# GLA and pooling decoder on one core: S as moving operand with its loads a step apart from its stores, first squares without GpSimd, one table set and r in PSUM at the end

## Chip, cores, metric

The kernel runs on one core of a Trainium2 chip. Measured is the device time of one launch in microseconds. TensorE is PE (PEld are its weight loads), VectorE DVE, ScalarE ACT, GpSimd POOL, and SyncE SP; SP issues all DMAs here.

## The reference, cut to what matters

Two layers of a decoder, for a prompt of 256 tokens and 8 samples of 8 tokens each, with the same weights. Everything is float32.

```python
def step(S, inp):                       # GLA, one chunk of the recurrence
    ...
    o_inter = einsum('bhid,bhdv->bhiv', qi * exp(b), S)
    k_dec = ki * exp(b_last - b)
    S_new = exp(b_last)[..., None] * S + einsum('bhjd,bhjv->bhdv', k_dec, vi)
    return S_new, o_intra + o_inter

def trunk(x, ...):
    for l in range(DEPTH):              # DEPTH = 2
        h = rmsnorm(x, norm_mix[l])
        m, s, b = mixer(h, ...)         # w_in, GLA (4 heads) and pooling, w_out
        x = x + m
        h = rmsnorm(x, norm_ffn[l])
        x = x + (silu(h @ w_gate[l]) * (h @ w_up[l])) @ w_down[l]
    return rmsnorm(x, norm_final), ...
```

For the samples each of 8 sequences has a state S of 128 x 256 per head, which is read (o_inter), decayed and added to, and written out; D_MODEL is 2048, D_FF 5632.

## The kernel before

**Layout.** Activations are transposed: channels on 128 partitions, the 320 tokens (256 of the prompt, 64 of the samples) along the free dimension; xT holds 16 such tiles of 320. Each weight value is split into a high and a low part of PE's fast float32 form (hl, two halves of the same tile), and so is the activation (xh, xl); `mm3` makes a product of three matmuls of 128 x 128 weights and 320 columns: high by high (L151), high by low (L152), low by high (L153).

**Units.** The program is a list of some 730 units. A unit is one weight tile of 128 x 1024 (512 KB): a load by SP into one of four raw buffers, a cast on ACT (L115) and a subtraction on DVE (L116) into one of three hl buffers, and eight `mm3`, that is 24 matmuls, on PE. `run` goes over the list: it loads up to five units ahead, splits two ahead, issues a unit's matmuls, then the evacuations due, then lets every generator in `gens` go one step. All engines get their instructions in that order, and each works through its own in order; SP's loads of weights, its loads of S and its stores stand in one queue.

**Small matmuls.** What the mixer needs beside the weight matmuls is queued by `add_small` with an estimated time, and `beside`, called after each `mm3`, puts small ones into the slots between; `placed` lets a generator wait until the queue is empty.

**Heads.** `head_gen` treats one head: loads of the two halves of S (four samples each; two buffers), transposes of v, then per half c of the 256 value channels a PSUM tile ps_o with the products of scores and v (L736, L738, for the samples L740) and, for each of the eight samples, one matmul with S as weights and that sample's eight columns of q8 moving (L743). Then come the new state (L719 into ps_sn, L728 on DVE, store L731), the sum of squares (L763), the prompt's state (L766) and the norm. Heads follow each other; `gate_gen` takes their o to the output projection. The PSUM pool sm has four buffers in turn for all these small tiles.

**Level stage.** Ahead of the heads, `gk_gen` and `level_gen` make the decays and the scores within the prompt; at s == 4 they make e8 = exp of the cumulated gate of the samples' tokens and q8 = e8 times q. `pool_gen` makes the pooling mixer, on POOL for the most part.

**Start.** `first_squares` forms the sum of squares of x over the 16 tiles, for the first norm: products and sums on POOL (L962, L963), two of the four chunks squared by ACT (L969). Meanwhile DVE makes the low parts of weights (L116) and of x (L119). A matmul with ones (ps_r) sums over partitions, and `rsqrt` makes r with Ln and Exp on ACT and four DVE instructions.

**End.** `finish` does the same for the last norm, with Ln's table loaded ahead and Exp's between the two, and multiplies the 16 tiles by r in six groups, four on DVE and two on POOL (L1017), each stored by SP (L1018).

Of the kernel before, what the change touches and what calls it, by code (L numbers as in the profile page):

```python
# [16 lines left out]
P = 128  # L17
# [49 lines left out]
class Decoder:  # L67
    def __init__(self, tc, ctx, a):
# [334 lines left out]
    def level_gen(self):  # L403
# [35 lines left out]
        for li, s in enumerate((1, 2, 4, 8, 16, 32, 64, 128)):  # L439
# [30 lines left out]
            if s == 4:  # L470

                nc.scalar.activation(st["e8"], P4[:, :, NP:T], AF.Exp, scale=1.0 / GKN)
                nc.vector.tensor_tensor(st["q8"], st["e8"], q4[:, :, NP:T], ALU.mult)
                self.gens.append(self.kd_sample())
# [191 lines left out]

    def head_gen(self, h, vT):
# [10 lines left out]
        S = []  # L678
        for qd in range(2):
            s = late.tile([P, 4, DV], F32, tag="S", name="S", bufs=2)  # L680
            nc.sync.dma_start(out=s, in_=a["s0"][l, h, :, 4 * qd : 4 * qd + 4])
            S.append(s)
# [28 lines left out]
        o = late.tile([P, 2, T], F32, tag="o", name="o", bufs=2)  # L711
        sq = late.tile([P, 2, T], F32, tag="osq", name="osq")
# [12 lines left out]
        def state_out(qd, pss):  # L725
            for b4 in range(4):
                b = 4 * qd + b4
                nc.vector.scalar_tensor_tensor(  # L728
                    S[qd][:, b4, :], S[qd][:, b4, :], st["e8"][:, h, 8 * b + 7 : 8 * b + 8],
                    pss[b4 // 2][:, 256 * (b4 % 2) : 256 * (b4 % 2) + 256], ALU.mult, ALU.add)  # L730
            nc.sync.dma_start(out=a["s_sample"][l, h, :, 4 * qd : 4 * qd + 4], in_=S[qd])  # L731

        def out_mm(c):
# [5 lines left out]
                po[:, 128:NP], vt[:, 1, vc], self.sc[:, h, 256:384], start=False, stop=True))  # L739
            self.add_small(220, lambda: nc.tensor.matmul(  # L740
                po[:, NP:T], vs[:, vc], self.scs[:, h, :], start=True, stop=False))
            for b in range(NB):
                self.add_small(224, lambda b=b: nc.tensor.matmul(  # L743
                    po[:, NP + 8 * b : NP + 8 * b + 8], S[b // 4][:, b % 4, vc],
                    st["q8"][:, h, 8 * b : 8 * b + 8], start=False, stop=(b == NB - 1)))
            return po

        def out(c, po):
            nc.scalar.activation(o[:, c, :], po[:, :T], AF.Copy, scale=self.vec(l, V_GN, c))
            nc.scalar.activation(sq[:, c, :], po[:, :T], AF.Square)  # L750

        pos = [out_mm(0), out_mm(1)]
        yield
        yield from self.placed()
        pss = state_mm(0)
        for c in range(2):
            out(c, pos[c])
# [5 lines left out]
        self.add_small(540, lambda: nc.tensor.matmul(pr[:, :T], self.ones, sq[:, 0, :], start=True, stop=True))  # L763
# [8 lines left out]
        nc.scalar.copy(sp, pS[:, :DV])
# [184 lines left out]
    def first_squares(self):  # L957
        nc = self.nc
        q = [self.ffb.tile([P, 8, T], F32, tag=t, name="q" + t) for t in ("ah", "al")]
        for c in range(2):  # L960
            x = self.xT[:, 4 * c : 4 * c + 4, :]
            nc.gpsimd.tensor_tensor(q[0][:, 4 * c : 4 * c + 4, :], x, x, ALU.mult)  # L962
        add = lambda a, b: nc.gpsimd.tensor_tensor(a, a, b, ALU.add)  # L963
        add(q[0][:, 0:4], q[0][:, 4:8])
        for c in range(2):
            for _ in range(2):
                yield
            v = q[1][:, 4 * c : 4 * c + 4]
            nc.scalar.activation(v, self.xT[:, 8 + 4 * c : 12 + 4 * c, :], AF.Square)  # L969
            if c == 0:  # L970
                add(q[0][:, 0:4], v)
                v = q[0]
            add(v[:, 0:2], v[:, 2:4])
            add(v[:, 0], v[:, 1])
# [27 lines left out]
    def finish(self, evacs):  # L1002
# [4 lines left out]
        nc.scalar.activation(self.warm, self.eps, AF.Ln)  # L1007
# [106 lines left out]
```

## Time and profile before

| | |
|---|---|
| median of 3 runs | 2707.62 us (2706.63 to 2709.3) |
| the profiled execution | 2707.78 us |
| its span | 2706.0 us, mean granted PE clock 0.996 |

Busy time of the engines by stage, in us, from the profile's stretches:

| stretch | length | PE | DVE | ACT | POOL |
|---|---|---|---|---|---|
| start, 0 to 60 | 60 | 53.44 | 44.53 | 32.12 | 21.35 |
| level stage of layer 0, 60 to 200 | 140 | 134.12 | 96.55 | 64.65 | 55.71 |
| heads, w_out, FFN of layer 0, 200 to 1350 | 1150 | 1150.00 | 546.08 | 440.20 | 85.12 |
| level stage of layer 1, 1350 to 1530 | 180 | 173.85 | 120.53 | 84.16 | 57.97 |
| the rest of layer 1, 1530 to 2680 | 1150 | 1150.00 | 534.59 | 438.73 | 83.83 |
| end, 2680 to 2706 | 26 | 9.09 | 11.29 | 7.79 | 6.67 |

PE's busy time counts pipelined matmuls, so full does not mean at its peak; what a matmul costs is read from the distance of its neighbours' starts. Records of f32 matmuls come in pairs: one instruction is two records. In rows of time the first two numbers are start and length in us, and the bracket at the end is the idle time ahead of the instruction with what ended it.

### The profile page before, as it was taken

Reading aid. Unit: us, or ns where it says so; the run is one execution under the profiler, and the core shown is the slowest. Engines: PE = TensorE matmul, PEld = TensorE weight load, DVE = VectorE, ACT = ScalarE, POOL = GpSimd, SP = SyncE. Lnnn points to the kernel's source line nnn. Section 1 sums busy time; section 2 is a strip of 40 time slices with the busy share of each in tenths; the row PEclk is TensorE's granted clock in tenths of the full one; section 3 lists DMA queues with packets and bytes.
Section 4 is the critical chain, followed back from the end, with each engine's and each line's share of the span. In section 5 each row is a group of like instructions: output and inputs, shape, how many; then the busy total and the mean of one; then the engine's idle time right before and its main releaser. Section 6 shows DMA issues by size and latency. Waiting matters only on the chain.

```text
span 2706.0 us, 44907 instructions
## 1 busy us (share of the span) xinstructions
PE 2670.5 (99%) x19046; PEld 2649.3 (98%) x19046; DVE 1353.6 (50%) x1662; ACT 1067.7 (39%) x1346; POOL 310.6 (11%) x347
## 2 busy tenths in 40 slices
PE   9999999999999999999999999999999999999997
PEld 8999999999999999999999999999999999999997
DVE  7754554544444444444658545445444444444444
ACT  5445544333333333333444554443333333333334
POOL 3521211000000000000106111100000000000002
PEclk9999999999999999999999999999999999999999
DMA  5455544444444444444443555544444444444443
GB/s 195 124 157 175 170 153 149 148 149 152 151 148 149 151 152 150 148 150 151 146 152 107 170 179 164 152 148 149 148 150 151 151 148 149 150 152 150 148 150 108
DMA packets 116217, 409.06 MB, mean 151 GB/s; under 512 B 13360, under 2 KB 16944, under 8 KB 116016
## 3 DMA queue, kind: packets, MB, share of 16 engines
q1 hardware_dynamic: 116016, 406.19, 47.9%
q8 instruction: 149, 2.44, 0.4%
q14 instruction: 52, 0.43, 0.0%
HBM read 392.98 MB, written 13.16 MB: 150 GB/s over the span
## 4 chain that ended last, share of the span: by engine, by line
PE 93%; issue 2%; DVE 2%; POOL 1%; ACT 1%; DMA 0%; DVEq 0%; SPq 0%; ACTq 0%; POOLq 0%
PE acc L151 31%; PE acc L153 30%; PE acc L152 30%; PE ps_o L743 1%; DVE hl L116 1%; POOL PX L466 0%; ACT hl L115 0%; POOL AS L615 0%; POOL AP L614 0%; PE ps_sn L719 0%; PE ps_o L736 0%; PE ps_sp L766 0%; PE ps_o L740 0%; DMA raw<-in_w_in 0%; DVE xT L1017 0%
## 5 line engine op out<-in xcount | busy, mean ns | idle before, releaser
L116 DVE TENSOR_TENSOR hl<-raw,hl 128x1024 fp32r<-128x1024 f32 (+1 forms) x729 | 923.3, 1267 | 1250.6 <-ACT hl L115 1249.6
L115 ACT CAST hl<-raw 128x1024 fp32r<-128x1024 f32 (+1 forms) x729 | 759.8, 1043 | 1291.1 <-PE acc L153 1244.4
L151 PE MATMUL acc<-xh,hl 128*128 128x320 f32 x3840 | 1212.0, 316 | 1.7 <-ACT xh L118 0.9
L153 PE MATMUL acc<-xh,hl 128*128 128x320 f32 x3840 | 1188.0, 309 | 4.2 <-DVE hl L116 4.2
L152 PE MATMUL acc<-xl,hl 128*128 128x320 f32 x3840 | 1187.4, 309 | 1.4 <-DVE xl L119 1.3
L151 PEld LDWEIGHTS acc<-xh,hl 128*128 128x128 f32 x3840 | 722.0, 188 | 6.8 <-issue 1.7
L153 PEld LDWEIGHTS acc<-xh,hl 128*128 128x128 f32 x3840 | 721.5, 188 | 5.9 <-DVE hl L116 5.6
L152 PEld LDWEIGHTS acc<-xl,hl 128*128 128x128 f32 x3840 | 722.4, 188 | 4.3 <-DVE xl L119 2.0
L153 PE MATMUL acc<-ah,hl 128*128 128x320 f32 x1408 | 435.1, 309 | 0.0
L151 PE MATMUL acc<-ah,hl 128*128 128x320 f32 x1408 | 435.1, 309 | 0.0
L152 PE MATMUL acc<-al,hl 128*128 128x320 f32 x1408 | 435.1, 309 | 0.0
L151 PEld LDWEIGHTS acc<-ah,hl 128*128 128x128 f32 x1408 | 264.3, 188 | 0.0
L152 PEld LDWEIGHTS acc<-al,hl 128*128 128x128 f32 x1408 | 264.3, 188 | 0.0
L153 PEld LDWEIGHTS acc<-ah,hl 128*128 128x128 f32 x1408 | 264.3, 188 | 0.0
L833 POOL TENSOR_TENSOR ft<-ft,r 128x320 f32<-128x320 f32 x88 | 75.4, 880 | 1641.2 <-ACT ft L832 1641.2
L275 DVE TENSOR_TENSOR xT<-xT,acc 128x320 f32<-128x320 f32 x224 | 98.4, 480 | 5.8 <-PE acc L153 5.8
L252 POOL TENSOR_TENSOR sqa<-sqa,sq 128x320 f32<-128x320 f32 x58 | 51.0, 879 | 289.6 <-ACT sq L251 287.5
L151 PE MATMUL acc<-ph,hl 128*128 128x320 f32 x256 | 80.4, 314 | 0.0
L152 PE MATMUL acc<-ol,hl 128*128 128x320 f32 x256 | 79.1, 309 | 0.0
L151 PE MATMUL acc<-oh,hl 128*128 128x320 f32 x256 | 79.1, 309 | 0.0
L153 PE MATMUL acc<-ph,hl 128*128 128x320 f32 x256 | 79.1, 309 | 0.0
L153 PE MATMUL acc<-oh,hl 128*128 128x320 f32 x256 | 79.1, 309 | 0.0
(202 smaller groups left out, 1572.8 us busy)
## 6 DMA issues: line engine op xcount, KB each, us to landing
raw<-in_w_gu SPq DMA_DIRECT2D x352, 512.0 KB, 3.6
raw<-in_w_down SPq DMA_DIRECT2D x176, 512.0 KB, 3.6
raw<-in_w_in SPq DMA_DIRECT2D x127, 512.0 KB, 4.0
raw<-in_w_out SPq DMA_DIRECT2D x64, 512.0 KB, 3.7
S<-in_s SPq DMA_DIRECT2D x16, 512.0 KB, 4.5
out_s_sample<-S SPq DMA_DIRECT2D x16, 512.0 KB, 3.3
raw<-in_w_pool SPq DMA_DIRECT2D x8, 256.0 KB, 2.9
xT<-in_xT SPq DMA_DIRECT2D x3, 640.0 KB, 7.3
```

The source lines that it names most:

```text
L115: nc.scalar.copy(hi, src)
L116: nc.vector.tensor_tensor(lo, src, hi.bitcast(F32), ALU.subtract)
L151: nc.tensor.matmul(ps, wh, xh, start=first, stop=False)
L152: nc.tensor.matmul(ps, wh, xl, start=False, stop=False)
L153: nc.tensor.matmul(ps, wl, xh, start=False, stop=last)
L252: nc.gpsimd.tensor_tensor(self.sq_acc, self.sq_acc, s, ALU.add)
L275: self.nc.vector.tensor_tensor(self.xT[:, m, :], self.xT[:, m, :], p, ALU.add)
L743: self.add_small(224, lambda b=b: nc.tensor.matmul(po[:, NP + 8 * b : NP + 8 * b + 8], S[b // 4][:, b % 4, vc], st["q8"][:, h, 8 * b : 8 * ...
L833: self.nc.gpsimd.tensor_tensor(t, t, self.r, ALU.mult)
```

## The change

**Heads.** q8 becomes a tile of its own, kept for the whole program, cleared once, with 32 columns for each of four samples of a half: the second half's eight columns stand eight further on. Four matmuls (`seq4`) take those 32 columns as weights and the four S tiles of a half as moving operand, 256 columns each, into four groups of 32 partitions of one PSUM tile ps_os. ACT copies it to qs, and per c one more matmul with qs as weights and a strided part of the identity moving adds it, transposed, into ps_o. Loads of S are issued by `load_state`: the first half of the next head a step after that half's store, the second half a step after its own.

**Start.** ACT squares all four chunks, DVE adds them up, ACT casts the masks.

**End.** The set that holds both Ln and Exp is loaded once ahead; r stands in PSUM for DVE, a copy of it for POOL; seven groups.

```diff
+        self.q8 = self.keep.tile([P, H, 4, 2, 32], F32, name="q8")
+        nc.gpsimd.memset(self.q8, 0.0)
...
             if s == 4:
-                nc.scalar.activation(st["e8"], P4[:, :, NP:T], AF.Exp, scale=1.0 / GKN)
-                nc.vector.tensor_tensor(st["q8"], st["e8"], q4[:, :, NP:T], ALU.mult)
+                e8 = early.tile([P, 640], F32, tag="Q", name="e8q", bufs=2)[:, :256].rearrange("p (h c) -> p h c", h=H)
+                nc.scalar.activation(e8, P4[:, :, NP:T], AF.Exp, scale=1.0 / GKN)
+                nc.scalar.copy(st["e8"], e8[:, :, 7::8])
+                for qd in range(2):
+                    c = slice(32 * qd, 32 * qd + 32)
+                    part = lambda t: t[:, :, c].rearrange("p h (j t) -> p h j t", j=4)
+                    nc.vector.tensor_tensor(self.q8[:, :, :, qd, 8 * qd : 8 * qd + 8], part(e8),
+                                            part(q4[:, :, NP:T]), ALU.mult)
...
+        def seq4(qd):
+            for j in range(4):
+                nc.tensor.matmul(os_[32 * j : 32 * j + 32, :], self.q8[:, h, j, qd, :], S[qd][:, j, :],
+                                 start=(qd == 0), stop=(qd == 1))
...
-            for b in range(NB):
-                self.add_small(224, lambda b=b: nc.tensor.matmul(
-                    po[:, NP + 8 * b : NP + 8 * b + 8], S[b // 4][:, b % 4, vc],
-                    st["q8"][:, h, 8 * b : 8 * b + 8], start=False, stop=(b == NB - 1)))
+            self.add_small(220, lambda: nc.tensor.matmul(po[:, NP:T], qs[:, vc], rows, start=False, stop=True))
...
         pos = [out_mm(0), out_mm(1)]
+        for qd in range(2):
+            self.add_small(430, lambda qd=qd: seq4(qd))
         yield
         yield from self.placed()
+        qs = late.tile([P, DV], F32, tag="qs", name="qs")
+        nc.scalar.copy(qs, os_)
         pss = state_mm(0)
         for c in range(2):
+            out_mm2(c, pos[c])
+        yield
+        yield from self.placed()
...
+        for c in range(2):
             out(c, pos[c])
-        nc.gpsimd.tensor_tensor(sq[:, 0, :], sq[:, 0, :], sq[:, 1, :], ALU.add)
+        nc.gpsimd.tensor_tensor(sq[0], sq[0], sq[1], ALU.add)
+        state_out(0, pss)
+        pss = state_mm(1)
         yield
         yield from self.placed()
-        state_out(0, pss)
+        if h + 1 < H:
+            self.load_state(l, h + 1, 0)
+        state_out(1, pss)
...
     def first_squares(self):
-        for c in range(2):
-            x = self.xT[:, 4 * c : 4 * c + 4, :]
-            nc.gpsimd.tensor_tensor(q[0][:, 4 * c : 4 * c + 4, :], x, x, ALU.mult)
-        add = lambda a, b: nc.gpsimd.tensor_tensor(a, a, b, ALU.add)
...
+        add = lambda a, b: nc.vector.tensor_tensor(a, a, b, ALU.add)
+        acc = q[0][:, 0:4]
+        for c in range(4):
+            v = q[c // 2][:, 4 * (c % 2) : 4 * (c % 2) + 4]
+            nc.scalar.activation(v, self.xT[:, 4 * c : 4 * c + 4, :], AF.Square)
...
-        nc.gpsimd.tensor_copy(self.masks, self.mf)
+        nc.scalar.copy(self.masks, self.mf)
...
     def finish(self, evacs):
-        nc.scalar.activation(self.warm, self.eps, AF.Ln)
+        nc.scalar.preload_act_table_set("natural_log_exp_and_others")
...
-        r = self.nrm.tile([P, T], F32, tag="r", name="fin_r", bufs=2)
-        self.rsqrt(r, ps, 1.0 / D_MODEL)
-        for lo, n, eng in ((0, 1, nc.vector), (11, 2, nc.gpsimd), (1, 3, nc.vector), (4, 4, nc.vector),
-                           (13, 3, nc.gpsimd), (8, 3, nc.vector)):
+        rp = self.smt("ps_finr")[:, :T]
+        rs = self.nrm.tile([P, T], F32, tag="r", name="fin_r", bufs=2)
+        self.rsqrt(rp, ps, 1.0 / D_MODEL)
+        nc.scalar.copy(rs, rp)
+        for lo, n, eng, r in ((0, 2, nc.vector, rp), (2, 3, nc.vector, rp), (12, 2, nc.gpsimd, rs),
+                              (5, 3, nc.vector, rp), (8, 2, nc.vector, rp), (14, 2, nc.gpsimd, rs),
+                              (10, 2, nc.vector, rp)):
```

PE's order in head 0 of layer 0, before, at the first matmul with S as weights (an instruction's line, operation, output and inputs, and its columns; an x at the end counts repeats):

```order
L740 MATMUL ps_o<-scs,vs 128x64
L151 MATMUL acc<-xh,hl 128x320
L152 MATMUL acc<-xl,hl 128x320
L153 MATMUL acc<-xh,hl 128x320
L743 MATMUL ps_o<-q_155,S 128x8
```

The same place now, where L154 to L156 are the former L151 to L153, from the first burst on to the matmuls of the new state:

```order
L751 MATMUL ps_os<-S,q_91 32x256 x4
L154 MATMUL acc<-xh,hl 128x320
L155 MATMUL acc<-xl,hl 128x320
L156 MATMUL acc<-xh,hl 128x320
L751 MATMUL ps_os<-S,q_91 32x256 x4
L154 MATMUL acc<-xh,hl 128x320
L155 MATMUL acc<-xl,hl 128x320
L156 MATMUL acc<-xh,hl 128x320
L154 MATMUL acc<-xh,hl 128x320
L155 MATMUL acc<-xl,hl 128x320
L156 MATMUL acc<-xh,hl 128x320
L729 MATMUL ps_sn<-vqt,kqt 128x512 x2
```

Sixteen slots with L743 per head have become two with four matmuls each, and the former L740 and the matmul with qs (L765 and L767) come after L729.

DVE's order in the first units, before (hl are low parts of weights, xl of x):

```order
L116 TENSOR_TENSOR hl<-raw,hl 128x1024 x2
L119 SCALAR_TENSOR_TENSOR xl<-xT,vecs,xh 128x320 x4
L116 TENSOR_TENSOR hl<-raw,hl 128x1024 x2
L119 SCALAR_TENSOR_TENSOR xl<-xT,vecs,xh 128x320 x4
L116 TENSOR_TENSOR hl<-raw,hl 128x1024
L983 TENSOR_REDUCE small<-ident 128x1
```

And now, with the sums of squares (L993, L1007):

```order
L119 TENSOR_TENSOR hl<-raw,hl 128x1024 x2
L993 TENSOR_TENSOR qah<-qah 128x1280
L122 SCALAR_TENSOR_TENSOR xl<-xT,vecs,xh 128x320 x4
L119 TENSOR_TENSOR hl<-raw,hl 128x1024
L993 TENSOR_TENSOR qah<-qah,qal 128x1280
L119 TENSOR_TENSOR hl<-raw,hl 128x1024
L122 SCALAR_TENSOR_TENSOR xl<-xT,vecs,xh 128x320 x4
L119 TENSOR_TENSOR hl<-raw,hl 128x1024
L993 TENSOR_TENSOR qah<-qah,qal 128x1280
L993 TENSOR_TENSOR qah<-qah 128x640
L1007 TENSOR_TENSOR sqa<-qah 128x320
```

The five sums stand between the splits, the first of them ahead of the xl of the third chunk of x.

ACT's order at the end, before:

```order
L1007 ACT_TABLE_LOAD
L1007 ACTIVATE small<-small 128x1
L903 ACTIVATE sq<-xT 128x320
L905 ACTIVATE xT<-xT,vecs 128x320
L903 ACTIVATE sq<-xT 128x320
L905 ACTIVATE xT<-xT,vecs 128x320
L139 ACTIVATE rs_t<-ps_fin,small 128x320
L140 ACT_TABLE_LOAD
L140 ACTIVATE rs_y<-rs_t 128x320
```

And now:

```order
L1036 ACT_TABLE_LOAD
L936 ACTIVATE sq<-xT 128x320
L938 ACTIVATE xT<-xT,vecs 128x320
L936 ACTIVATE sq<-xT 128x320
L938 ACTIVATE xT<-xT,vecs 128x320
L142 ACTIVATE rs_t<-ps_fin,small 128x320
L143 ACTIVATE rs_y<-rs_t 128x320
L1044 COPY fin_r<-ps_finr 128x320
```

The second table load is gone from between the two functions, and the copy for POOL has come behind them.

More of the change, by code (lines that the diff above doesn't have):

```diff
@@ L665, in ev_v, with load_state @@
         self.gens.append(self.head_gen(h, vT))
+    def load_state(self, l, h, qd):
+        s = self.late.tile([P, 4, DV], F32, tag="S", name="S", bufs=2)
+        self.nc.sync.dma_start(out=s, in_=self.a["s0"][l, h, :, 4 * qd : 4 * qd + 4])
+        self.st.setdefault("S", {}).setdefault(h, []).append(s)
     def head_gen(self, h, vT):
@@ L677, in head_gen @@
             yield
[L678 to L682, printed above, removed]
+        if h == 0:
+            self.load_state(l, 0, 0)
+        self.load_state(l, h, 1)
+        S = st["S"].pop(h)
         p1, p2, p3 = self.smt("ps_vt"), self.smt("ps_vs"), self.smt("ps_vq")
@@ L767, in head_gen @@
                 pS[:, :DV], st["kdt"][:, t, 128 * h : 128 * h + 128], vt[:, t, :], start=(t == 0), stop=(t == 1)))
-        pss = state_mm(1)
         yield
         yield from self.placed()
-        sp = late.tile([P, 2, T], F32, tag="osq", name="sp")[:, 0, :DV]
+        sp = late.tile([P, DV], F32, tag="qs", name="sp")
         nc.scalar.copy(sp, pS[:, :DV])
         nc.sync.dma_start(out=a["s_prompt"][l, h], in_=sp)
-        state_out(1, pss)
-        ro = late.tile([P, T], F32, tag="ro", name="ro")
+        ro = self.nrm.tile([P, T], F32, tag="sqa", name="ro")
         self.rsqrt(ro, pr[:, :T], 1.0 / DV)
@@ L959, in first_squares @@
         q = [self.ffb.tile([P, 8, T], F32, tag=t, name="q" + t) for t in ("ah", "al")]
-        for c in range(2):
-            x = self.xT[:, 4 * c : 4 * c + 4, :]
-            nc.gpsimd.tensor_tensor(q[0][:, 4 * c : 4 * c + 4, :], x, x, ALU.mult)
[L963 to L966, printed above, removed]
-                yield
[L968 to L974, printed above, removed]
+        add = lambda a, b: nc.vector.tensor_tensor(a, a, b, ALU.add)
[3 more added lines that the diff above has]
+            nc.scalar.activation(v, self.xT[:, 4 * c : 4 * c + 4, :], AF.Square)
+            if c == 0:
+                nc.gpsimd.memset(self.sc, 0.0)
+                nc.gpsimd.memset(self.scs, 0.0)
+            else:
+                add(acc, v)
+            for _ in range((1, 1, 2, 0)[c]):
+                yield
+        add(acc[:, 0:2], acc[:, 2:4])
         self.sq_acc = self.nrm.tile([P, T], F32, tag="sqa", name="sqa")
-        nc.gpsimd.tensor_tensor(self.sq_acc, q[0][:, 0], q[1][:, 4], ALU.add)
-        nc.gpsimd.memset(self.sc, 0.0)
-        nc.gpsimd.memset(self.scs, 0.0)
+        nc.vector.tensor_tensor(self.sq_acc, acc[:, 0], acc[:, 1], ALU.add)
         while self.mf is None:
             yield
-        nc.gpsimd.tensor_copy(self.masks, self.mf)
+        nc.scalar.copy(self.masks, self.mf)
         nc.vector.tensor_reduce(self.low, self.ident.rearrange("p (g c) -> p g c", c=32)[:, :, LR:],
```

21 lines of the change are left out of this document (12 added, 9 removed).

## The prediction

> **What bounds the kernel now.** I read the page first (span, engines, the chain that ended last), then the stretches in which PE (TensorE) has idle time, then PE's own order of time in the heads.
>
> ```profile
> span 2706.0 us, 44907 instructions
> PE 2670.5 (99%) x19046; PEld 2649.3 (98%) x19046; DVE 1353.6 (50%) x1662; ACT 1067.7 (39%) x1346; POOL 310.6 (11%) x347
> PE 93%; issue 2%; DVE 2%; POOL 1%; ACT 1%; DMA 0%; DVEq 0%; SPq 0%; ACTq 0%; POOLq 0%
> ```
>
> PE is busy 99% of the span, and 93% of the chain that ended last is its matmuls (third line). So a matmul taken out between the weight matmuls shortens the program by its whole slot, and on the other engines only what makes PE wait counts: the start, two spots of the level stage, and the end. Three parts of the change touch just these. The sum is made against the profiled execution, 2707.78 us, which lies 0.16 us over the median of the runs (2707.62).
>
> **Heads: S as moving operand.** PE in time in head 0 (start, length, line):
>
> ```profile
> 187.88 0.31 PE L153 MATMUL acc<-xh,hl 128*128 128x320 f32 x1
> 188.03 0.59 PE L736 MATMUL ps_o<-sc,vt 128*128 128x256 f32 x2
> 188.75 0.31 PE L153 MATMUL acc<-xh,hl 128*128 128x320 f32 x1
> 189.41 0.31 PE L153 MATMUL acc<-xh,hl 128*128 128x320 f32 x1
> 189.65 0.43 PE L740 MATMUL ps_o<-scs,vs 64*128 64x64 f32 x2
> 190.41 0.31 PE L153 MATMUL acc<-xh,hl 128*128 128x320 f32 x1
> 190.56 0.28 PE L743 MATMUL ps_o<-q,S 128*128 128x8 f32 x2
> ...
> 194.62 0.31 PE L153 MATMUL acc<-xh,hl 128*128 128x320 f32 x1
> ```
>
> and its group, all heads of both layers (records, busy time, mean ns):
>
> ```profile
> L743 PE MATMUL ps_o<-q,S 128*128 128x8 f32 x256 | 35.2, 219 | 0.0
> ```
>
> Matmuls overlap, so a price is the distance between two L153, less 0.44 us for the three weight matmuls in it; these follow each other in 0.147 us, as in the first row and the next, 188.03 - 187.88. From 190.41 to 194.62 stand six such threes and seven L743: 4.21 - 2.64 = 1.57, so 0.224 us each. The group row counts 256 records, two per instruction: 128 instructions. **Removed: 128 x 0.224 = 28.7 us.**
>
> Added are 16 matmuls L767 (qs through part of the identity, weights 128x128, 64 columns). L743 has the same weights with 8 columns and costs 0.224; L738, the only other matmul between 188.75 and 189.41, has 128 columns and costs 0.66 - 0.44 = 0.22. Between equal ends: 16 x 0.22 = 3.6 us.
>
> Added are also 16 bursts L751: four matmuls with 32 weight columns each, to four groups of 32 output partitions, 256 columns of S moving. The only large ones of this form are L375's:
>
> ```profile
> 47.34 0.31 PE L153 MATMUL acc<-xh,hl 128*128 128x320 f32 x1
> 47.58 2.36 PE L375 MATMUL ps_gk<-xT,gkw 128*32 128x320 f32 x32
> ...
> 50.27 0.31 PE L153 MATMUL acc<-xh,hl 128*128 128x320 f32 x1
> ```
>
> That is 16 instructions, four rounds over the four groups, in 2.93 - 0.44 = 2.49 us. One 256-column f32 matmul alone (L736) costs 188.75 - 187.88 - 0.44 = 0.43, so one of 320 costs 0.54 and 16 in a row 8.6: the four groups do run side by side. Four rounds of 0.54 are 2.15; the rest, 0.35, is either paid once per burst or spread over the rounds. A one-round burst of 256 columns then costs between 2.49 / 4 x 0.8 = 0.50 (spread) and 0.43 + 0.35 = 0.78 (once); its far end, with no overlap, is 4 x 0.43 + 0.35 = 2.07, and no reason puts it under the 0.43 of one stream. I take 0.65, the middle of the two readings of the same row: **16 x 0.65 = 10.4 us** (8.0 to 12.5). Heads: -28.7 + 3.6 + 10.4 = **-14.7 us**.
>
> L740, with 64 rows of weights, costs 190.41 - 189.41 - 0.44 = 0.56 where the larger L738 costs 0.22: leaving the full 128x128 form has a price here, once per visit. The Trainium skill, page "TensorEngine Tiling (Array Packing)", section "Tiling Modes", says that changing the tiling mode drains the engine; it speaks against bursts strewn singly among full matmuls. By that rule the whole rest is paid per burst; L740's row agrees in sign.
>
> The new waits in the heads. The copy qs (ACT) must be done before the second L729 of the next unit, which takes over a PSUM buffer, and before L767; everything on PE is queued behind. Between the second burst and that matmul stand two threes and a first L729, 1.1 us by the distances above.
>
> ```profile
> L772 ACT COPY sp<-ps_sp x8: 372/373/373, 211.5 to 1649.7; 128x256 f32<-128x256 f32 x8
> L749 ACT ACTIVATE o<-ps_o,vecs x16: 508/524/528, 200.8 to 1640.6; 128x320 f32<-128x320 f32 x16
> ```
>
> A copy of that size takes 0.37 (first row), so 0.7 us are left for hand-over; ACT's cast before it waits for an earlier unit and is long done. Likewise the second pair of ps_sn waits for o and its square, four instructions of about 0.5, the last of which can start some 2.8 us before it is needed. I charge nothing, and up to 0.5 us per head, 4 us, in the range. The loads of S move on SP: now each waits for a store issued a step before. In before both stood directly behind the store.
>
> ```profile
> SPq L681 <- DMA out_s_sample<-S: 8.1, 3, 4.0
> ```
>
> SP waited there up to 4.0 us, three times in layer 0, and no PE idle time stands in the heads. Nothing gained, nothing lost. By the order on PE a head now takes six units instead of seven (the last one seven), so what waits for o in the output projection has more room.
>
> **Start: squares without GpSimd.** PE in time, with its waits:
>
> ```profile
> 10.70 0.64 PE L152 MATMUL acc<-xl,hl 128*128 128x320 f32 x1 [1.30 <-DVE xl L119]
> 20.13 0.42 PE L153 MATMUL acc<-xh,hl 128*128 128x320 f32 x1 [1.34 <-DVE hl L116]
> 28.91 0.41 PE L153 MATMUL acc<-xh,hl 128*128 128x320 f32 x1 [1.48 <-DVE hl L116]
> ```
>
> DVE, POOL and ACT in the same part, one stretch of it by engine (its last three numbers are granted clock, DMA share and GB/s), and a sum of 1280 elements on DVE from later:
>
> ```profile
> 5.73 0.69 DVE L116 TENSOR_TENSOR hl<-raw,hl 128x512 fp32r<-128x512 f32 x1 [4.74 <-ACT hl L115]
> 6.34 1.01 DVE L119 SCALAR_TENSOR_TENSOR xl<-xT,vecs,xh 128x320 fp32r<-128x320 f32 x2
> 8.51 1.68 DVE L116 TENSOR_TENSOR hl<-raw,hl 128x512 fp32r<-128x512 f32 x1 [1.16 <-ACT hl L115]
> 21.13 6.58 DVE L119 SCALAR_TENSOR_TENSOR xl<-xT,vecs,xh 128x320 fp32r<-128x320 f32 x4
> 20.90 3.14 POOL L963 TENSOR_TENSOR qah<-qah,qal 128x1280 f32<-128x1280 f32 x1 [3.70 <-ACT qal L969]
> 32.44 1.06 ACT L115 CAST hl<-raw 128x1024 fp32r<-128x1024 f32 x1 [3.03 <-PE acc L153]
> 11.13:13.80 2.67, 2.67 (x12) 2.67 (x11) 2.67 (x1) 2.64 (x5) 2.59 (x2) 0.50 1.02 421
> L399 DVE TENSOR_TENSOR PX<-PX x2: 1492/1492/1493, 63.9 to 1399.7; 128x1280 f32<-128x1280 f32 x2
> ```
>
> While POOL works DVE crawls: 1.68 against 0.69 for the same split, four xl in 6.58 against two in 1.01. Three PE waits end on that. Without POOL the second split ends 1 us earlier, its first xl at about 9.8, and the wait at 10.70 shrinks from 1.30 to about 0.45. DVE takes over three sums of 1280 (1.49 each by L399), one of 640 and one of 320, some 5.7 us, but the chunk at 21.13 alone gives back 4.5 us. Walking DVE's new row with these prices, the third chunk's xl ends near 21 and the split behind it near 22, where PE needs them about 24: 2 us of cover, and the first chunk has more. So both waits go: 0.85 + 1.34 + 1.48 = **-3.7 us**. If the cover fails, the larger two stay (gain 0.85); ACT's two more squares and the mask cast lie in the 3 us for which its next cast waits on PE anyway (32.44); the mask's load, for which ACT would now hold its queue, is issued earlier too, since the splits that free SP's buffers are. POOL is left with memsets that nothing waits for.
>
> From 11.13 to 13.80 the granted clock was 0.50, and PE set off some ten matmuls where at 0.147 us there would be eighteen. The Trainium skill, page "TensorE: Matmul & The Clock Gate", section "What's actually happening", has the clock set by how busy PE was in windows of 3.4 us. The row's stretch fits one such window. With less idle time the low stretch might vanish, which by that row is worth half of 2.67, some 1.2 us. I leave it in the range.
>
> **Level stage.** Its one long PE wait per layer:
>
> ```profile
> 119.23 0.39 PE L151 MATMUL acc<-dh,hl 128*128 128x320 f32 x1 [3.14 <-DVE ES L596]
> L473 DVE TENSOR_TENSOR q<-e,qk x2: 1552/1554/1555, 107.8 to 1443.5; 128x256 f32<-128x256 f32 x2
> ```
>
> q8 becomes two DVE instructions, ACT gets a small copy, and the next Q now waits for q8. All lie 11 us ahead of this wait, on the engines that it ends on. Split halves cost at least their start, at most another 1 us per layer; I take 0.25 each: **+0.5 us**.
>
> **End: one table set, r in PSUM.**
>
> ```profile
> 2689.74 1.28 ACT L140 ACT_TABLE_LOAD   x1
> 2693.11 7.38 DVE L1017 TENSOR_TENSOR xT<-xT,fin_r 128x320 f32<-128x320 f32 x4
> 2693.15 4.92 POOL L1017 TENSOR_TENSOR xT<-xT,fin_r 128x640 f32<-128x640 f32 x2 [10.04 <-DVE fin_r L144]
> 2703.00:2704.00 1.00, 0.00 (x0) 0.00 (x0) 0.00 (x0) 0.00 (x0) 0.00 (x0) 0.50 1.00 403
> 2704.00:2705.00 1.00, 0.00 (x0) 0.00 (x0) 0.00 (x0) 0.00 (x0) 0.00 (x0) 0.50 0.33 123
> L595 DVE TENSOR_TENSOR EP<-acc,r x16: 408/417/420, 93.4 to 1494.0; 128x256 f32<-128x256 f32 x16
> ```
>
> (The two stretch rows end like the one above.) The load between Ln and Exp goes: 1.28 us on the path, and r, which released both multipliers at 2693.11, is ready at 2691.8. DVE's eleven chunks of 320 took 7.38 beside POOL; L595, which reads PSUM, stays between 0.41 and 0.42 in all 16 cases, some beside POOL. So twelve chunks cost by L399's rate about 4.5 us and end at 2696.3. Then the output is what is late: 16 x 320 floats in 128 rows are 2.62 MB, at 403 GB/s 6.5 us, from about a microsecond after the first product (2693.7) to 2700.2; in before the last bytes moved at 2704.3 (a third of that stretch). **-4.0 us**. Bounds: DVE still beside POOL, 1.5; transfers hidden, 5.
>
> **Sum.** -14.7 - 3.7 + 0.5 - 4.0 = -21.9: 2685.9 from the profiled run, 2685.7 for a median; I say **2686**.
>
> **Rivals.**
> 1. The rest is paid in every burst, by the switch of form that L740 shows: heads -12.6, time 2688. L375's four rounds cannot tell. Chance 0.15.
> 2. The start keeps its waits, now behind DVE's sums: 2689. For it: the sums stand ahead of the very xl that PE waits for; against: 4.5 us freed at one chunk. 0.09.
> 3. DVE and POOL still hinder each other at the end: 2688.5. Against it stands L595. 0.06.
> 4. The change doesn't do what it says: bursts run one matmul after the other, 16 x 2.07 = 33 us, heads +8, time 2708, or 2703 with no fixed part. L375 against it. No difference. 0.05.
> 5. Slower: SP. Each load of S waits for a store, twice per head change, 12 times, and the weight loads queue behind. If each hit PE with the 4.0 us of the row, 48 us, the time would be 2734. It eats the whole gain from 1.8 us of lost PE time per wait (21.9 / 12), and the kernel is slower by 0.2% from 2.3. Against it: the same 4.0 cost PE nothing. 0.02.
>
> Forecast 0.6; the rest, 0.03, mixtures. 0.2% is 5.4 us, about what a measurement of this kernel can tell from no change. Faster 0.93, same 0.05, slower 0.02. The range takes the low ends of the burst, the clock and the transfers (2680) and the high ends of burst, start and end together (2694).
>
> **What would show it.** PE: bursts L751 with 0.5 to 0.78 us of extra distance between their L156; no PE wait on L756 or qs. Start: ps_r some 3.7 us earlier, no waits at the second and third chunk, four xl in 2.0. End: one table load after the last weight matmul, DVE multiplications done 4.5 us after r, last byte 8.5 us after. Wrong would be bursts over 1 us, PE waits in the heads, or a level wait grown by more than 1 us.

## The result, and the profile after

| | before | after |
|---|---|---|
| median | 2707.74 us of 4 runs (2706.63 to 2709.3) | 2687.36 us of 4 runs (2686.65 to 2687.84) |
| ratio, 95% interval | | 0.9924 (0.9907 to 0.9941) |
| the profiled execution, its span | 2707.78, 2706.0 | 2687.01, 2685.1 |

The kernel is 0.76% faster. The page of the changed kernel, the lines that answer to those of before:

```profile
span 2685.1 us, 44741 instructions
PE 2654.4 (99%) x18950; PEld 2623.4 (98%) x18950; DVE 1344.8 (50%) x1670; ACT 1073.4 (40%) x1358; POOL 294.3 (11%) x338
PE 94%; issue 2%; DVE 2%; POOL 1%; ACT 1%; DMA 1%; SPq 0%; DVEq 0%; ACTq 0%; POOLq 0%
```

PE is still the bound, with 16 us less to do and less idle time. Where the 20.9 us of span went is read from the starts of the same PE matmuls in both traces:

| PE's first matmul of | before | after | earlier by | step between the marks |
|---|---|---|---|---|
| ps_r, the first norm | 35.76 | 30.00 | 5.76 | start -5.76 |
| ps_vt, head 0 of layer 0 | 179.89 | 174.83 | 5.06 | level stage +0.70 |
| ps_r, behind w_out of layer 0 | 428.28 | 416.73 | 11.55 | heads -6.49 |
| ps_vt, head 0 of layer 1 | 1515.89 | 1505.02 | 10.87 | level stage +0.68 |
| ps_r, behind w_out of layer 1 | 1764.27 | 1746.92 | 17.35 | heads -6.48 |
| ps_fin, the last norm | 2687.05 | 2669.70 | 17.35 | 0 |
| end of the span | 2706.0 | 2685.1 | 20.9 | end -3.55 |

**Heads.** PE in time around the two bursts of head 0, layer 0 (start, length, line):

```profile
186.31 0.31 PE L156 MATMUL acc<-xh,hl 128*128 128x320 f32 x1
186.55 0.64 PE L751 MATMUL ps_os<-S,q 128*32 128x256 f32 x8
...
187.51 0.31 PE L156 MATMUL acc<-xh,hl 128*128 128x320 f32 x1
187.75 0.64 PE L751 MATMUL ps_os<-S,q 128*32 128x256 f32 x8
...
188.72 0.31 PE L156 MATMUL acc<-xh,hl 128*128 128x320 f32 x1
```

A burst costs 1.20 - 0.44 = 0.76 in the first slot, 0.77 in the second. That is near the upper of the prediction's two readings of L375 (0.78), the one in which the rest is paid once per visit; experiment 3 tests this. (The sixteen L743 of a head stood in fourteen slots before, not sixteen: two of the slots took two.) The five longest of PE's nine waits in the whole program (total, times, longest):

```profile
PE acc L154 <- DVE ES L604: 6.3, 2, 3.3
PE acc L154 <- DVE pl L136: 3.5, 2, 1.9
PE acc L154 <- ACT xh L121: 2.0, 2, 1.0
PE ps_kq L573 <- DVE Ds L495: 1.7, 2, 1.0
PE acc L156 <- DVE hl L119: 1.4, 2, 0.7
```

None of the nine lines names qs, ps_os, S or o: nothing in the heads makes PE wait. All five shown belong to the start and the level stages.

**Start.** PE's waits in the first 32 us, behind the 1.05 us at its very first matmul, which are the same in both kernels:

```profile
6.31 0.41 PE L154 MATMUL acc<-xh,hl 128*128 128x320 f32 x1 [0.98 <-ACT xh L121]
7.04 0.42 PE L155 MATMUL acc<-xl,hl 128*128 128x320 f32 x1 [0.31 <-DVE xl L122]
9.06 0.42 PE L154 MATMUL acc<-xh,hl 128*128 128x320 f32 x1 [1.00 <-ACT xh L121]
9.79 0.41 PE L155 MATMUL acc<-xl,hl 128*128 128x320 f32 x1 [0.31 <-DVE xl L122]
```

The waits at the second and third chunk of x (at 20.13 and 28.91 before) are gone. PE is 2.42 earlier behind the first chunk, 1.60 more at the next, 1.74 more at the last.

**Level stage.** The wait for ES is as it was; the one behind it, for Ds, has grown from 0.33 to 0.99 in layer 0. Its chain in the changed kernel, from POOL over SP and DVE to PE:

```profile
105.06 2.90 POOL L634 COPY so<-EP 128x30 f32<-128x30 f32 x1
```

```profile
107.99 0.35 SPq L636 DMA_DIRECT2D out_pool_out<-so  x1
...
108.86 0.46 SPq L600 DMA_DIRECT2D stg<-in_bufT  x1
```

```profile
114.81 1.53 DVE L470 TENSOR_TENSOR PX<-PX 128x512 f32<-128x512 f32 x1 [1.17 <-POOL PX L468]
```

```profile
118.20 0.63 PE L573 MATMUL ps_kq<-ident,kq 128*128 128x128 f32 x4 [0.99 <-DVE Ds L495]
```

And the same copy, the same two DMAs and the same two waits before:

```profile
111.14 0.71 POOL L626 COPY so<-EP 128x30 f32<-128x30 f32 x1
```

```profile
111.88 0.35 SPq L628 DMA_DIRECT2D out_pool_out<-so  x1
...
112.74 0.45 SPq L592 DMA_DIRECT2D stg<-in_bufT  x1
```

```profile
120.01 1.53 DVE L468 TENSOR_TENSOR PX<-PX 128x512 f32<-128x512 f32 x1 [0.47 <-POOL PX L466]
```

```profile
123.41 0.63 PE L565 MATMUL ps_kq<-ident,kq 128*128 128x128 f32 x4 [0.33 <-DVE Ds L487]
```

With the program 5.8 us earlier, the store and the load of stg behind it are only 3.9 us earlier: POOL's copy of 30 columns took 2.90 in place of 0.71. The load of stg landed at 113.15, and POOL could copy out of it at 113.28; before it had landed at 116.83, well ahead of POOL's copy at 118.08. PE's own wait is a poor measure of this, because it also depends on how early PE gets there: in two further profiles of the kernel before (experiment 10) the wait for Ds in layer 0 is 1.73. The distance from the matmul that ES releases to the end of DVE's Ds is steady: 4.15 and 4.14 us in the two layers before, 4.85 and 4.55 now, so 0.70 and 0.41 are lost there.

**End.** Last instructions on DVE, ACT and POOL, and three stretches of a microsecond (the last three numbers: granted clock, DMA share, GB/s):

```profile
2673.96 0.50 DVE L147 SCALAR_TENSOR_TENSOR ps_finr<-rs_t,rs_y 128x320 f32<-128x320 f32 x1
2674.49 0.42 ACT L1044 COPY fin_r<-ps_finr 128x320 f32<-128x320 f32 x1 [1.62 <-DVE ps_finr L147]
2674.95 4.41 DVE L1049 TENSOR_TENSOR xT<-xT,ps_finr 128x640 f32<-128x640 f32 x5 [0.49 <-ACT fin_r L1044]
2674.99 3.05 POOL L1049 TENSOR_TENSOR xT<-xT,fin_r 128x640 f32<-128x640 f32 x2 [9.21 <-ACT fin_r L1044]
```

```profile
2676.00:2677.00 1.00, 0.00 (x0) 0.00 (x0) 1.00 (x2) 0.00 (x0) 1.00 (x2) 0.76 0.36 138
...
2679.00:2680.00 1.00, 0.00 (x0) 0.00 (x0) 0.36 (x1) 0.00 (x0) 0.00 (x0) 0.50 1.06 406
...
2683.00:2684.00 1.00, 0.00 (x0) 0.00 (x0) 0.00 (x0) 0.00 (x0) 0.00 (x0) 0.50 0.52 197
```

DVE's twelve tiles take 4.41, the transfers then run at about 400 GB/s to 2683.5, 9.05 after r. DVE's first product waited 0.49 for ACT's copy of r, though both only read it: the instruction carries a wait on ACT in the program.

### The profile page after: what moved, and what is told of

It is laid out like the page before. It is cut to its first block, busy times and chain, and to the rows that moved or that the text cites. A ratio compares the mean times of both kernels' runs of the same rounds, so it can differ in the third digit from the quotient of the medians.

```text
span 2685.1 us, 44741 instructions
## 1 busy us (share of the span) xinstructions
PE 2654.4 (99%) x18950; PEld 2623.4 (98%) x18950; DVE 1344.8 (50%) x1670; ACT 1073.4 (40%) x1358; POOL 294.3 (11%) x338
## 3 DMA queue, kind: packets, MB, share of 16 engines
q8 instruction: 148, 2.42, 0.4%
## 4 chain that ended last, share of the span: by engine, by line
PE 94%; issue 2%; DVE 2%; POOL 1%; ACT 1%; DMA 1%; SPq 0%; DVEq 0%; ACTq 0%; POOLq 0%
PE acc L154 31%; PE acc L156 30%; PE acc L155 30%; DVE hl L119 1%; POOL PX L468 0%; PE ps_os L751 0%; DMA stg<-in_bufT 0%; POOL AS L623 0%; POOL AP L622 0%; PE ps_sn L729 0%; PE ps_sp L801 0%; PE ps_o L757 0%; PE ps_o L765 0%; POOL so L634 0%; ACT hl L118 0%
## 5 line engine op out<-in xcount | busy, mean ns | idle before, releaser
L154 PE MATMUL acc<-xh,hl 128*128 128x320 f32 x3840 | 1206.5, 314 | 2.8 <-ACT xh L121 2.0
L156 PE MATMUL acc<-xh,hl 128*128 128x320 f32 x3840 | 1187.1, 309 | 1.4 <-DVE hl L119 1.4
L154 PEld LDWEIGHTS acc<-xh,hl 128*128 128x128 f32 x3840 | 721.0, 188 | 15.4 <-issue 8.3
L156 PEld LDWEIGHTS acc<-xh,hl 128*128 128x128 f32 x3840 | 720.8, 188 | 2.7 <-DVE hl L119 2.5
L156 PE MATMUL acc<-ah,hl 128*128 128x320 f32 x1408 | 435.1, 309 | 0.0
L154 PE MATMUL acc<-ah,hl 128*128 128x320 f32 x1408 | 435.1, 309 | 0.0
L154 PEld LDWEIGHTS acc<-ah,hl 128*128 128x128 f32 x1408 | 264.3, 188 | 0.0
L156 PEld LDWEIGHTS acc<-ah,hl 128*128 128x128 f32 x1408 | 264.3, 188 | 0.0
L154 PE MATMUL acc<-ph,hl 128*128 128x320 f32 x256 | 79.1, 309 | 0.0
L155 PE MATMUL acc<-pl,hl 128*128 128x320 f32 x256 | 79.1, 309 | 0.0
L156 PE MATMUL acc<-ph,hl 128*128 128x320 f32 x256 | 79.1, 309 | 0.0
L154 PE MATMUL acc<-oh,hl 128*128 128x320 f32 x256 | 79.1, 309 | 0.0
```

What stands on the lines that cost most here:

```text
L154: nc.tensor.matmul(ps, wh, xh, start=first, stop=False)
L155: nc.tensor.matmul(ps, wh, xl, start=False, stop=False)
L156: nc.tensor.matmul(ps, wl, xh, start=False, stop=last)
```

## Experiments

Single times of one kernel spread over a microsecond or two, so parts of a microsecond are read from the positions of the same PE matmuls, as in the table above. For the heads and the end these agree within some hundredths between profiles of one kernel. For a level stage they don't: against the first profile of the kernel before, two further ones (experiment 10) are 0.2 to 0.4 shorter in layer 0 and 1.7 and 2.2 longer in layer 1, with nothing changed. There the distance from ES to Ds is used as well.

**1. The heads alone.** The changed kernel with `first_squares` and `finish` as they were before.

> Only the part with S as moving operand (q8 in its own tile, bursts, loads a step apart); start and end as in the kernel before. In the trace of the change, PE's position against before moves by -5.76 us in the start, +0.69 in each level stage, -6.5 in the heads of each layer, and -3.55 behind the first matmul of the last norm. Theory (the parts add up): here 0 at the start, +0.7 after each level stage, -6.5 in each layer's heads, so -11.6 at ps_fin, 0 at the end, time 2707.7 - 11.6 = 2696. Rival (the level stage's +0.7 is not q8's but comes of the earlier start, which shifts it against POOL and the DMA queue): 0 after each level stage, -13.0 at ps_fin, time 2694.7.

Measured: 2695.54 us, ratio 0.9952 (0.9935 to 0.9969). Heads -6.48 and -6.47; level stages +0.03 and +0.56; the end, from ps_fin on, the 18.95 us of before. The parts add up, and ps_fin is 11.66 earlier, as expected, but partly by luck: the start of this execution was 0.71 slower than in the first profile of before, and the level stages lost 0.59 in place of 1.4. What the level stage loses without the earlier start is seen from ES to Ds: 4.51 and 4.44 us, so 0.36 and 0.30 more than before. The same copy of so takes 2.91 in both layers here. So the loss comes with this part of the change, where q8 is what the level stage has that is new.

**2. The start alone.** The kernel before with the new `first_squares`.

> Only the first squares without GpSimd; the rest as in the kernel before. Theory (the start's gain is the change's own, clock included): ps_r 5.8 us earlier than before, that offset kept to the end, time 2707.7 - 5.8 = 2702; no PE wait at the second and third chunk. Rival A (part of the first chunk's 2.4 us is the phase of the clock's windows, which differs from one execution to the next): the profile shows a stretch of 0.50 again within the first 15 us, ps_r is about 4.2 earlier, time 2703.5. Rival B for the level stage (its +0.7 per layer comes of the earlier start): +0.7 after each level stage here too, time 2703.4, with ps_r still 5.8 earlier.

Measured: 2702.22 us, ratio 0.9977 (0.9967 to 0.9986). In the profile ps_r is 4.37 earlier, not 5.76, and there is a stretch of 0.50 in the clock: rival A's numbers, for this execution (2703.07). The median of the ten runs is the theory's 2702; they reach from 2700.76 to 2704.51. No wait at the two later chunks. Level stages -0.13 and -0.17, copy of so 0.71, from ES to Ds 4.16 in both layers: rival B falls. The clock's part is taken up by experiment 10.

**3. Both bursts in one slot.**

```diff
-        for qd in range(2):
-            self.add_small(430, lambda qd=qd: seq4(qd))
+        self.add_small(860, lambda: (seq4(0), seq4(1)))
```

> The changed kernel with both bursts of a head (eight matmuls of 32 weight columns) in one slot in place of two. In the change one burst adds 0.76 us to its slot. Theory (a fixed part of about 0.33 is paid once for a visit, 0.43 for each round): the slot with both lasts 0.44 + 0.33 + 2 x 0.43 = 1.63 between the two L156 around it, in place of two of 1.20; 0.34 less per head, 2.7 in all, 2684.7. Rival (each round costs 0.76, in one visit or in two): the slot lasts 1.96, time 2687.4 as the change.

```profile
185.82 0.31 PE L156 MATMUL acc<-xh,hl 128*128 128x320 f32 x1
186.05 1.07 PE L751 MATMUL ps_os<-S,q 128*32 128x256 f32 x16
...
187.46 0.31 PE L156 MATMUL acc<-xh,hl 128*128 128x320 f32 x1
```

Measured: 2684.44 us, ratio to before 0.9912 (0.9897 to 0.9927). The slot lasts 1.64, so eight matmuls cost 1.20 where two bursts cost 1.53: 0.33 is paid per visit, 0.43 per round. Head 1 starts 28.58 behind head 0, in the change 28.89; 2.5 us in eight heads. The theory stands, the price per round falls.

**4. L765 with 128 rows.** vs and scs are kept in 128 rows, the upper 64 zero.

```diff
-        self.scs = self.keep.tile([64, H, 64], F32, name="scs")
+        self.scs = self.keep.tile([P, H, 64], F32, name="scs")
...
+        self.vs = self.late.tile([P, DV], F32, tag="vs", name="vs")
+        self.nc.gpsimd.memset(self.vs, 0.0)
...
-        nc.scalar.copy(vs, p2[:64, :DV])
+        nc.scalar.copy(vs[:64], p2[:64, :DV])
```

> The changed kernel with vs and scs held in 128 rows, the upper 64 zero, so that the matmul L765 has 128 rows of weights like its neighbours; vs is cleared once per layer. Theory (leaving the full form costs about 0.34 per visit, whichever smaller form it is): the slot of L765 falls from 1.00 to 0.66, 16 x 0.34 = 5.4 us, time 2682. Rival (L765's price belongs to its place or its operands, not to the 64 rows): slot 1.00 as before, time 2687.4.

L767 of this kernel is the former L765 (scs and vs), now between two matmuls L156:

```profile
191.36 0.30 PE L156 MATMUL acc<-xh,hl 128*128 128x320 f32 x1
191.50 0.33 PE L767 MATMUL ps_o<-scs,vs 128*128 128x64 f32 x2
...
192.01 0.31 PE L156 MATMUL acc<-xh,hl 128*128 128x320 f32 x1
```

Measured: 2681.23 us, ratio to before 0.9901 (0.9886 to 0.9916). The slot is 0.65 in place of 1.00, with the same 64 columns and twice the rows. Heads lie 28.22 apart, 0.67 less each, 5.4 us in all. Zeros are cheaper than a smaller form. The Trainium skill, page "TensorEngine Tiling (Array Packing)", section "Tiling Modes", says that a change of mode drains TensorE; experiments 3 and 4 agree in that a visit has a price, 0.33 to 0.35 us here.

**5. Loads of S back at the head's start.**

```diff
-        if h == 0:
-            self.load_state(l, 0, 0)
+        self.load_state(l, h, 0)
         self.load_state(l, h, 1)
...
-        if h + 1 < H:
-            self.load_state(l, h + 1, 0)
```

> The changed kernel with both loads of S of a head issued at the head's start, directly behind the stores of the head before, as in the kernel before. Theory (the step apart is worth nothing on PE's path): SP waits longer at L677 than the 2.4 us of the change, up to about 4.0, PE waits for no S, heads -6.5 per layer as in the change, time 2687.4. Rival (six units per head leave too little room, so the step apart is what keeps the bursts from waiting for S): PE waits for S in three heads of each layer, some 2 to 4 us each, time 2700 to 2710.

Measured: 2686.83 us, ratio to before 0.9922 (0.9907 to 0.9937), and not one hundredth of a microsecond of difference in the heads' distances. In one point the expectation missed: SP does not wait longer for the stores of S, but not at all. Placed a step apart the loads wait 13.4 us in seven places, up to 2.4. Neither reaches PE.

**6. The store of so a step later.** On SP the load of stg then no longer stands behind it.

```diff
-        nc.sync.dma_start(out=self.a["pool_out"][l, i], in_=so)
+        def store():
+            nc.sync.dma_start(out=self.a["pool_out"][l, i], in_=so)
+            yield
+        self.gens.append(store())
```

> The changed kernel with the store of so (pool_out) one step later on SP, behind the load of stg. Theory (the level stage lost time because the two halves of q8 on DVE hold up POOL's copies of so, the store of so on SP and with it the load of stg queue behind them, and POOL's PX, DVE's PX and Ds follow): DVE's wait for POOL's PX goes from 1.17 back to about 0.5, PE's wait for Ds from 0.99 to about 0.4, each level stage 0.5 less, 1.0 in all, 2686.4. Rival (DVE itself is late by the second half of q8, or the difference is where windows of low clock fall): no change at Ds, 2687.4.

SP, DVE and PE at the places shown above:

```profile
105.44 0.35 SPq L600 DMA_DIRECT2D stg<-in_bufT  x1
108.09 0.35 SPq L638 DMA_DIRECT2D out_pool_out<-so  x1
```

```profile
114.20 1.54 DVE L470 TENSOR_TENSOR PX<-PX 128x512 f32<-128x512 f32 x1 [0.47 <-POOL PX L468]
```

```profile
117.59 1.08 PE L573 MATMUL ps_kq<-ident,kq 128*128 128x128 f32 x4 [0.67 <-DVE Ds L495]
```

Measured: 2685.55 us, ratio to before 0.992 (0.9903 to 0.9936); level stages 0.74 and 0.54 shorter than in the change. These two lengths alone prove little, as other profiles with the change's level stage are up to 0.67 and 0.69 shorter than the change's own. DVE's wait for POOL's PX is back at 0.47 and 0.46, and from ES to Ds it takes 4.15 and 4.14 us. So it was in both layers of all four profiles without the new q8 (4.14 to 4.16), and so it is in experiment 11 with this edit (4.15 twice); the eight profiles with the new q8 and the old place of the store have 4.28 to 4.85, on average 0.40 too much. POOL's copy still takes 2.90, so it is the queue behind it on SP that carried the delay to Ds. The theory holds, with PE's wait at 0.67 rather than 0.4 in layer 0 and none left in layer 1.

**7. The last multiplication on DVE alone.** No copy of r, no POOL, groups of 1, 2, 3, 3, 3, 2, 2 tiles.

> The changed kernel with all 16 tiles of the last multiplication on DVE with r in PSUM, no copy of r and no POOL, first group of one tile. In the change DVE's first product waits 0.49 for ACT's copy of r, and its first group of two takes some 0.8. Theory (the output's transfer, 2.62 MB at about 400 GB/s, is the bound, and starts when the first product is stored): first store 0.5 + 0.4 earlier, the rest follows at the transfer's pace, end 0.9 earlier, 2686.5; DVE's 16 tiles at 0.37 take 5.9, less than the 6.6 of the transfer. Rival (both engines are needed to feed the transfer): DVE's last product comes 5.9 after r in place of 4.9, the end 0.5 to 1 later, 2688.

```profile
2673.62 5.88 DVE L1045 TENSOR_TENSOR xT<-xT,ps_finr 128x320 f32<-128x320 f32 x7
```

Measured: 2686.24 us, ratio to before 0.9919 (0.9904 to 0.9934). From ps_fin to the end 14.84 in place of 15.39: 0.55 earlier, 0.9 expected. DVE starts right behind r (2673.58), the 0.49 is gone, and its 16 tiles take 5.88 as priced; from 2675 to 2677 the transfers run at only 269 and 323 GB/s, which is likely the missing part. POOL isn't needed there.

**8. r of the last norm in SBUF.**

> The changed kernel with r of the last norm in SBUF for both engines, no copy; still one table set and the same seven groups. Theory (DVE with both operands in SBUF is held up beside POOL: 0.67 a tile before, 0.37 now from PSUM): DVE's 12 tiles take about 7 us beside POOL, POOL's some 5, the transfer runs dry, the end 1.5 to 2 later, 2689.2; the table alone gave the other 1.3 of the 3.55. Rival (no contention from r's place): DVE 0.37 a tile, and 0.5 less for the copy that is gone: 2686.9.

```profile
2675.05 7.10 DVE L1047 TENSOR_TENSOR xT<-xT,fin_r 128x640 f32<-128x640 f32 x5
2675.16 4.51 POOL L1047 TENSOR_TENSOR xT<-xT,fin_r 128x640 f32<-128x640 f32 x2 [8.81 <-DVE fin_r L147]
```

Measured: 2688.85 us, ratio to before 0.9928 (0.9913 to 0.9943). From ps_fin to the end 16.60, so 1.21 later than in the change, though 0.49 of waiting is gone: DVE's twelve tiles take 7.10 in place of 4.41, POOL's four 4.51 in place of 3.05. The theory's sign and cause hold, its 1.5 to 2 was a little high.

**9. The sums of the first squares on POOL.**

> The changed kernel with the five sums of the first squares on POOL in place of DVE (ACT still squares all four chunks). Theory (what PE lost at the second and third chunk in the kernel before was DVE being held up while POOL works): two xl take more than the 1.0 us again beside POOL, PE waits again at the second and third chunk, 1.6 and 1.7 us in before against none in the change, so ps_r up to 3.3 later than in the change, by at least 1.5, and the time 2689 to 2690.7. Rival (before lost it by the length of POOL's own chain of squares, not by holding DVE up): no waits at these chunks, ps_r within 0.5 of the change apart from a stretch of 0.50 in the granted clock, 2687.4.

DVE's low parts of the third chunk of x in the change, then those of the third and fourth chunk here, two of POOL's sums and PE's wait:

```profile
18.43 1.93 DVE L122 SCALAR_TENSOR_TENSOR xl<-xT,vecs,xh 128x320 fp32r<-128x320 f32 x4
```

```profile
17.19 6.99 DVE L122 SCALAR_TENSOR_TENSOR xl<-xT,vecs,xh 128x320 fp32r<-128x320 f32 x4 [0.40 <-ACT xh L121]
...
26.38 6.53 DVE L122 SCALAR_TENSOR_TENSOR xl<-xT,vecs,xh 128x320 fp32r<-128x320 f32 x4
```

```profile
16.78 2.97 POOL L993 TENSOR_TENSOR qah<-qah 128x1280 f32<-128x1280 f32 x1 [13.51 <-ACT qah L997]
20.77 3.06 POOL L993 TENSOR_TENSOR qah<-qah,qal 128x1280 f32<-128x1280 f32 x1 [1.01 <-ACT qal L997]
```

```profile
25.37 0.41 PE L156 MATMUL acc<-xh,hl 128*128 128x320 f32 x1 [2.60 <-DVE hl L119]
```

Measured: 2690.24 us, ratio to before 0.9931 (0.9913 to 0.9949). Four xl take 6.99, in the change 1.93, and PE waits again, once and longer rather than twice; a stretch of 0.50 in the clock follows, and ps_r is 3.75 later, of which 2.86 lie at the wait. Adding on POOL alone brings the trouble back. The Trainium skill, page "SBUF — State Buffer", section "Who interferes with whom", says that a DVE instruction with two inputs in SBUF contends with a GpSimd instruction that reads SBUF, and that one locks the other out; experiments 8 and 9 agree, 7.10 against 4.41 and 6.99 against 1.93, and POOL's copy of 2.90 would be the same on the other side.

**10. The kernel before, twice more, for the clock in its start.**

> The kernel before, once more, for its start. Of nine profiles with the new start, six show no stretch of 0.50 within the first 15 us (ps_r at 29.5 to 30.0) and three show one (ps_r at 31.2 to 31.4); both profiles with the old start show one or more (ps_r at 35.8 and 36.5). Theory (the low stretch follows PE's idle time in a window, and the old start has more of it, so the change removes it in most executions): a stretch of 0.50 here too, ps_r at 35.5 to 36.5. Rival (the phase alone decides, two times in three without): no such stretch, ps_r at about 34.2.

> As the run before it, a second look at the same kernel: theory, a stretch of 0.50 within the first 15 us and ps_r at 35.5 to 36.5; rival, no such stretch and ps_r at about 34.2.

Single runs, 2708.97 and 2709.0 us; ps_r at 35.63 and 35.02. The mean granted clock from 4 to 18 us was 0.76 and 0.63; 0.88 in the first profile of before and 0.70 in experiment 1, which has the same start. With the new start it was 1.00 in the change and in experiments 3, 5, 6, 7 and 11, 0.88 in 2, 4 and 8. So the old start showed the low stretch 4 times of 4, the new one 3 of 9. Two successive windows of the kernel before, of the change, and of experiment 2 (PE's busy time is the second number, the granted clock the third from the end):

```profile
7.25:10.66 3.41, 1.24 (x6) 0.75 (x5) 2.25 (x4) 2.49 (x4) 2.32 (x1) 1.00 1.02 411
10.66:14.07 3.41, 3.37 (x13) 3.37 (x14) 3.41 (x2) 2.87 (x5) 3.04 (x2) 0.50 1.02 419
```

```profile
7.29:10.70 3.41, 2.10 (x12) 1.57 (x12) 2.04 (x5) 2.47 (x4) 0.00 (x0) 1.00 1.00 392
10.70:14.11 3.41, 3.41 (x25) 3.41 (x24) 3.18 (x6) 3.27 (x6) 0.00 (x0) 1.00 1.02 421
```

```profile
6.92:10.34 3.42, 2.15 (x11) 1.62 (x11) 2.12 (x5) 2.48 (x4) 0.00 (x0) 1.00 0.98 377
10.34:13.75 3.41, 3.41 (x15) 3.41 (x14) 3.08 (x5) 2.85 (x6) 0.00 (x0) 0.50 1.03 423
```

A window with 1.24 of 3.41 us busy is followed by half clock; with 2.1 it may go either way. All fourteen profiles agree, up to the last norm, if each is cut into windows of 3.41 us on which its low stretches lie: a window at full clock with at most 1.57 us of PE busy was followed by half clock 32 times of 32, one with 1.62 to 2.29 us 4 times of 46, and one with 2.32 us or more never. The theory holds in most: the new start lifts PE's share to where the low stretch is no longer certain. What decides in between stays open.

**11. Four edits together** (3, 4, 6 and 7).

> The changed kernel with four of the edits above: both bursts in one slot, L765 with 128 rows, the last multiplication on DVE alone, the store of so a step later. Theory (they lie in different places, and PE is busy throughout the heads): by PE's positions -2.5, -5.4, -0.55 and -1.3 add up to -9.7, time 2677.6. Rival (a head shorter by 1 us leaves o, qs or S no cover any more): a PE wait on qs, po or S in the heads, and less than 8 gained, 2680 or more.

Measured: 2677.99 us, ratio to before 0.9885 (0.9871 to 0.99). Heads lie 27.90 apart, 0.99 less each, level stages 0.35 and 0.43 shorter, from ps_fin to the end 14.85; span 2675.7, 9.4 less than the change. PE waits for nothing in the heads. The edits add up, and this version beats both kernels.

## Why the prediction held, point by point

The forecast was 2686, the time 2687.36: direction, range and the places were right. By its own terms, of the profiled execution, it was out by +1.1 in all (2685.9 against 2687.01). That it came so close is partly luck, because larger errors of both signs met: heads +1.7, level stages +0.9 and end +0.5 against -2.1 in the start.

- **Heads, -14.7 forecast, -12.97 measured.** Mechanism right, one term mis-sized: "I take 0.65, the middle of the two readings of the same row". A burst costs 0.765 on average, 16 x 0.765 = 12.2 in place of 10.4. The rest is paid once per visit (experiment 3), which was rival 1's price; its -12.6 is near what the heads show. The other terms stand: L767 is 0.66 - 0.44 = 0.22 as priced (16 of them are 3.5 us, where the prediction wrote 3.6), and -28.7 + 3.5 + 12.2 = -13.0 gives back the measured sum. Charging nothing for qs, o and the loads of S was right (PE's waits, experiment 5).
- **Start, -3.7 forecast, -5.76 measured.** The two later chunks gave 1.60 and 1.74 for 1.34 and 1.48: right, and due to POOL being out of DVE's way (experiment 9). At the first chunk 0.85 became 2.42, since the stretch of 0.50 was gone, which was left to the range at up to 1.2. Where it comes back the start gains 4.4 (experiment 2). In the sum it would have belonged with its odds. What a low stretch costs the old start can't be read, as all four profiles have one; it seems little, since PE then waits less for DVE at the later chunks (ps_r lies between 35.0 and 36.5 over clocks of 0.63 to 0.88, the earliest at the lowest clock). With the new start ps_r is some 1.4 later where the stretch comes back.
- **Level stage, +0.25 per layer forecast, +0.69 measured in this pair of profiles.** Of it 0.70 and 0.41 lie at Ds, and 0.40 on average over the eight profiles; the rest is within what the stage varies. The step that failed: "All lie 11 us ahead of this wait, on the engines that it ends on." The wait for ES hardly moved (3.14 to 2.99 and 3.04 to 3.28). A small copy on POOL is held up in both layers of all ten profiles with the new q8 (2.90 to 2.92, without it 0.70 to 0.71), with the early start or without it; the copy held up a store on SP, a load queued behind the store, and Ds came late 11 us on (experiments 1, 2, 6). That the two halves of q8 on DVE are what moves the copy is argued from the order of the rows, and not tested by itself. I had followed DVE and ACT, and not what POOL and SP hand on.
- **End, -4.0 forecast, -3.55 measured.** The table load was worth 1.26 (r comes 6.02 behind ps_fin before, 4.76 after), and DVE's twelve tiles took 4.41 for 4.5, thanks to r in PSUM (experiment 8). Last byte 9.05 after r where 8.5 was forecast: the 0.49 for the copy, a wait that I had not priced.
- **Rivals.** The first was right for its term, and not for the total, as the start made up for it. The second falls (no wait at the later chunks), the third by experiment 8 (it is true of SBUF, not of PSUM), the fourth by the bursts' 0.76, the fifth because PE waits for none of the loads that SP delays by 13.4 us in all.

## What to carry to other kernels

On a PE-bound kernel count visits, not only matmuls: both small forms tried between full 128 x 128 matmuls here (32 columns of weights, 64 rows of weights) paid about a third of a microsecond for going there and back, so group such matmuls in one slot, or fill them up with zeros. Follow an instruction that is made longer on DVE to POOL, and from POOL to the DMA queue behind its stores, even if these have slack. Where a later norm or sum runs on DVE and POOL side by side, put the shared operand in PSUM, or leave POOL out.

## What the hardware showed that was not expected

- A matmul with 64 rows of weights and 64 moving columns cost 0.56 us between full ones, the same with 128 rows, half of them zero, 0.22.
- DVE's first read of r in PSUM waited 0.49 us for ACT's copy, which only reads the same tile; with the copy gone DVE started at once (experiment 7). The wait stands in the program; whether the chip would need it was not tried.
- A POOL copy of 30 columns took 2.90 us beside a row of DVE instructions that have two operands in SBUF (Q, K, d), ending with the last of them (107.96 and 107.89), and 0.71 before, at another moment of the same row. Spans on POOL are rough, but SP's store behind it came late as well.
- The clock fell to 0.50 for whole stretches of 3.41 us, or two or three of them, after stretches in which PE had been busy for as much as 2.29 of 3.41 us, so without a stretch of full idleness (the counts stand in experiment 10). The Trainium skill, page "TensorE: Matmul & The Clock Gate", section "What's actually happening", has windows of this length that run freely, and lets the clock fall after an idle window. These traces show the length, and low stretches that begin at other times in each execution of one kernel (at 10.66, 8.04 and 7.61 us in the three profiles of the kernel before); but here a partly busy window was enough.
